# Down projection of a hybrid decoder layer: the low weight part from an accumulating GpSimd DMA in place of a VectorE subtraction

## Chip, cores and metric

One core of a Trainium2 chip runs the whole layer. The metric is the device time of one execution in microseconds (us); lower is better. "Before" is the kernel without the change.

## What is computed

The reference is one decoder layer over 512 tokens of width 1024 in float32: two attention branches with gates, an output projection, a gated MLP with a causal convolution, and per-layer embeddings. The change touches the MLP's last product, whose weight `w_down` is 2816 x 1024:

```
h = rmsnorm(x, mlp_pre_norm[i])
u = causal_dwconv(h @ w_up[i], conv_w[i], conv_b[i])
u_gate, u_val = jnp.split(u, 2, axis=-1)
ff = (jax.nn.gelu(u_gate, approximate=True) * u_val) @ w_down[i]
x = x + rmsnorm(ff, mlp_post_norm[i])
e = p[i] @ w_ple[i]
x = x + jax.nn.sigmoid(rmsnorm(x, ple_norm[i]) @ w_ple_gate[i]) * e
```

## The kernel before

Every large product is made in three passes of a reduced-precision type (fp32r): each operand is written as hi + lo, and `mm3` (line 75) issues hi*hi, hi*lo and lo*hi into the same bank of PSUM. An operand is split by `split` (line 71): ScalarE copies the float32 source into an fp32r tile (hi, line 72), and VectorE subtracts hi from the source into another fp32r tile (lo, line 73).

Weights come in chunks of 128 partitions x 1024 float32 (512 KB). `chunk` (line 133) takes a raw buffer, has SyncE (SP) issue the load (line 137), takes a hi and a lo buffer and calls `split`. The buffers stand in rings that are taken in turn (`wtile`, line 120): from line 672 on there are 3 raw, 4 hi and 4 lo buffers (lines 117 and 672 together). A raw buffer can be loaded again once its lo is made, since VectorE reads it; a hi or lo buffer can be written again once TensorE has made its last product with the chunk that was in it. Up projection, down projection and the gate of the embeddings all draw on these rings.

The down projection (`down_pass`, line 814) walks 11 chunks in each of three passes. Pass 0 makes the first 512 output columns for four blocks of 128 tokens: a chunk serves 2 x 4 x 3 = 24 products. Pass 1 makes the other 512 columns for blocks 0 and 1, pass 2 the same columns for blocks 2 and 3; each loads its 11 chunks anew, and there a chunk serves 12 products. So 33 chunks of `wd` are loaded. After pass 1 the norm of blocks 0 and 1 (`post_norm`, line 703) runs beside pass 2: ScalarE squares, VectorE scales and adds, and GpSimd makes the power of -1/2 (lines 710 and 102). `to_hT` (line 720) then transposes the blocks for the gate product, whose weights `wpg` come through `chunk` again (lines 837 and 840).

A scheduler orders each engine's instructions by priorities and its own estimate of time; on the chip each engine then works through its queue in that order, and an instruction that waits holds up all those behind it on its engine. GpSimd issues no DMA in this kernel.

Of the kernel before, what the change touches and what calls it, by code (L numbers as in the profile page):

```python
# [8 lines left out]
F32 = mybir.dt.float32  # L9
F32R = mybir.dt.float32r  # L10
I32 = mybir.dt.int32
AF = mybir.ActivationFunctionType
ALU = mybir.AluOpType
PSUM = bass.MemoryType.PSUM

P = 128
# [4 lines left out]
NPAIR = DFF // P  # L21
# [7 lines left out]

# columns of the per-partition parameter array  # L30
PP_QA, PP_KVA, PP_BG, PP_W0, PP_W1, PP_W2, PP_CB = 0, 2, 3, 19, 63, 107, 151
PP_N = 195
# columns of the constant array
CS_ID, CS_ONE, CS_SWA, CS_CAU, CS_INV = 0, 128, 256, 512, 1024
# [3 lines left out]
def hybrid_kernel(ctx, tc, T):  # L38
    nc = tc.nc
    act, dve, pool = nc.scalar, nc.vector, nc.gpsimd  # L40
    order = mybir.DependencyInfo(mybir.DependencyClass.NoSync, mybir.DependencyReason.DATA)

    class pe:
        """Products into one tile of PSUM keep their order."""
        last = {}
# [17 lines left out]
    def opened(**kw):  # L63
        cm = tc.tile_pool(reuse_waits="tile", **kw)
        p = cm.__enter__()
        return p, lambda: cm.__exit__(None, None, None)

    def f32(ap):
        return ap.bitcast(F32)

    def split(hi, lo, src):
        act.activation(hi, src, AF.Copy)  # L72
        dve.tensor_tensor(lo, src, f32(hi), ALU.subtract)  # L73
# [9 lines left out]

# [1 line left out]
    cpool, close_cpool = opened(name="cpool", bufs=1, side="left")  # L85
# [17 lines left out]

# [1 line left out]
    xp, close_xp = opened(name="xp", bufs=1, side="right")  # L105
# [9 lines left out]

    # rings of weights: pools with their buffers of each kind, taken in turn
    RA = (wa, {"raw": 2, "hi": 3, "lo": 2})
# [9 lines left out]

    # what is left of the first weights, then the outputs of the sliding window
    yt = yp.tile([P, 4, 1024], F32R, name="yt", tag="yt")
# [3 lines left out]
    def chunk(src, n=1024, parts=1, dst=None):  # L133
        raw = wtile("raw" if not W["slots"] or (W["raw"] + W["lo"]) & 2 == 0 else "lo", F32)
        w = n // parts
        for i in range(parts):
            nc.sync.dma_start(raw[:, i * w:(i + 1) * w], src[:, i * w:(i + 1) * w])
        hi = dst[0] if dst else wtile("hi", F32R)
        if dst:
            lo = dst[1]  # L140
        elif W["slots"]:
            lo = W["slots"].pop(0)
            W["slots"].append(lo)
        else:
            lo = wtile("lo", F32R)
        if parts == 1:
            split(hi[:, :n], lo[:, :n], raw[:, :n])
        else:
            for i in range(parts):
                u = slice(i * w, (i + 1) * w)  # L150
                dve.tensor_copy(hi[:, u], raw[:, u])
                dve.tensor_tensor(lo[:, u], raw[:, u], f32(hi[:, u]), ALU.subtract)
        return hi, lo

    def work(name="wkt"):
        return wk.tile([P, 1280], F32, name=name, tag="wkt", bufs=3)
# [13 lines left out]

# [1 line left out]
    psp, close_psp = opened(name="psp", bufs=1, space=PSUM)  # L172
# [11 lines left out]

    # the clock of the tensor engine rises while the first loads are on their way
    zeros = work("zeros")
    dve.memset(zeros[:, :P], 0.0)
    for _ in range(WARM):
        pe.matmul(psB[3][:, :P], zeros[:, :P], zeros[:, :P], start=True, stop=True)
    for k in range(8):  # L190
# [5 lines left out]
        if k % 2 == 0:  # L196
            hi, lo = chunk(T["wC"][k // 2], 768, 2 if k == 0 else 1)
        proj(psC, hi, lo, k, k % 2, 384)
    chB = [chunk(T["wB"][c], 576) for c in range(2)]
    nc.sync.dma_start(pp, T["pp"])  # L200
    # sigmoid(z) = (1 + tanh(z / 2)) / 2
    hb = cpool.tile([P, 16], F32, name="hb")
# [7 lines left out]

    # rstd of x, by token
    ssx = cpool.tile([P, NB], F32, name="ssx")
    rstd = cpool.tile([P, NB], F32, name="rstd")
# [3 lines left out]

# [1 line left out]
    posf = cpool.tile([P, NB], F32, name="posf")  # L219
# [25 lines left out]
    def rope(src, h, w, c, s2, a, b):  # L245
        """a + b is src (P, h, 2, w) rotated; c (P, w), s2 (P, 2, w)."""
        dve.tensor_tensor(a, src, c.unsqueeze(1).unsqueeze(1).to_broadcast([P, h, 2, w]), ALU.mult)
        for hf in range(2):
            dve.tensor_tensor(b[:, :, hf, :], src[:, :, 1 - hf, :],
                              s2[:, hf:hf + 1, :].to_broadcast([P, h, w]), ALU.mult)  # L250

    # rstd along the free axis, on every partition
    rbc = cpool.tile([P, S], F32, name="rbc")

    # q: rotate, transpose, split and stack
    St = sp.tile([P, 8, S], F32R, name="St", tag="sp")
# [18 lines left out]

    # k duplicated over the halves of the partitions
    khl = kvp.tile([P, 2, 2, S], F32R, name="khl", tag="kva")
# [32 lines left out]

# [1 line left out]
    def a_chunk(c):  # L312
# [3 lines left out]

    # norms of the latents
    ssc = cpool.tile([P, 2, NB], F32, name="ssc")
# [19 lines left out]

# [1 line left out]
    for c in range(4):  # L340
        hi, lo = chB[c] if c < 2 else chunk(T["wB"][c], 576)
# [8 lines left out]
    for t in range(3):  # L350
# [5 lines left out]
        dve.scalar_tensor_tensor(cqT[1][:, t, :], pt, g, f32(cqT[0][:, t, :]), ALU.mult, ALU.subtract)  # L356
    # rotary part of q, by token
    hi, lo = chunk(T["wuqp"], 512)
    qps = []
    for n in range(NB):  # L360
        ps = scT("psqp")
        b = slice(n * P, (n + 1) * P)
        for k in range(2):
            w = slice(k * 256, (k + 1) * 256)
# [6 lines left out]
    a_chunk(1)  # L371
    # rstd broadcast
    dg = work("dg")
# [23 lines left out]

# [1 line left out]
    ga = kvp.tile([P, 8, S], F32, name="ga", tag="ga")  # L399
# [33 lines left out]
    kT = qkp.tile([P, 8, S], F32, name="kT", tag="kT")[:96]  # L433
    # queries and keys of the latents: parts without rotation, transposed
    def latent_k(g):
# [21 lines left out]

    # shared rotary key: transpose, one copy for every head
    def latent_kr():
# [23 lines left out]

    # sliding window: a step is a block of queries and a kv head
    def swa_scores(n, g):
# [44 lines left out]

    # one pair of passes: the parts of v side by side, their outputs on the halves of the partitions
    def pv_mms(out, v, h, l, start, stop):
# [16 lines left out]

    # latent attention: a step is a head  # L550
    OFF = (0, 128, 384, 768)
# [58 lines left out]

    # values of the latent branch, by token
    vb = []
# [31 lines left out]

# [1 line left out]
    mxh = xp.tile([P, 8, S], F32R, name="mxh", tag="xh")  # L646
# [8 lines left out]
    for m in range(8):  # L655
# [3 lines left out]
        hi, lo = ch_b  # L659
        pb = p3[m]("pb")  # L660
        for k in range(4):
            w = slice((m % 2) * S + k * P, (m % 2) * S + (k + 1) * P)
# [14 lines left out]

# [1 line left out]

    pairs = [[accT, accT], [ptT, ptT], [scT, scT], [scT, pvT]]  # L680
# [59 lines left out]
    for blocks in ((0, 1), (2,), (3,)):  # L740
# [4 lines left out]
        if blocks == (2,):  # L745
            to_hT(0, ts[0])
            to_hT(1, ts[1])
# [1 line left out]
    ff = [xp.tile([P, 8, S], F32R, name="ff" + t, tag="x" + t) for t in "hl"]  # L749
# [23 lines left out]

    # the first two pairs by halves of the tokens
    chs = {j: [chunk(T["wup"][2 * j + gv]) for gv in range(2)] for j in range(2)}
# [22 lines left out]
    for j in range(2, NPAIR):  # L798
        if j in (8, 16):
            if j == 16:  # L800
                fp, close_fp = opened(name="fp", bufs=1, side="left")
            for l, t in ((ffh, "kT"), (ffl, "qT")):
                w = min(8, NPAIR - j)
# [10 lines left out]
    def down_pass(half, blocks):  # L814
        for c in range(NPAIR // 2):
            hi, lo = chunk(T["wd"][half * (NPAIR // 2) + c])
            for kk in range(2):
                k = 2 * c + kk
                w = slice(kk * S, (kk + 1) * S)
                for n in blocks:  # L820
                    b = slice(n * P, (n + 1) * P)
                    mm3(yd[n][half], ffh[k][:, b], ffl[k][:, b], hi[:, w], lo[:, w], k == 0, k == NPAIR - 1)
# [11 lines left out]

# [1 line left out]
    close_fp()  # L836
# [45 lines left out]
    raw = lp.tile([P, 1024], F32, name="wraw", tag="wraw", bufs=2)  # L882
    nc.sync.dma_start(raw, T["pT"].rearrange("p a b -> p (a b)"))
    split(ph.rearrange("p a b -> p (a b)"), pl.rearrange("p a b -> p (a b)"), raw)
    for k in range(2):
        raw = lp.tile([P, 1024], F32, name="wraw", tag="wraw", bufs=2)
        nc.sync.dma_start(raw, T["wp"][k])
        split(wph[:, k, :], wpl[:, k, :], raw)
    for n in range(NB):
        b = slice(n * P, (n + 1) * P)  # L890
        for half in range(2):
            ps = bank(2 + n % 2, "pe")
            w = slice(half * S, (half + 1) * S)
# [18 lines left out]
def layouts(i):  # L912
    """The inputs as the program takes them: slices, transposes and packing alone."""
    f = lambda a: np.ascontiguousarray(a)
    x = np.asarray(i["x"])[0]
# [5 lines left out]
    two = lambda w: w.reshape(4, 2, P, -1).transpose(0, 2, 1, 3).reshape(4, P, -1)  # L921
# [7 lines left out]
    wd = np.asarray(i["w_down"])[0].reshape(NPAIR // 2, 2, P, 2, 512).transpose(3, 0, 2, 1, 4)  # L929
# [5 lines left out]
    q, k = np.arange(P)[:, None], np.arange(P)[None, :]  # L935
# [64 lines left out]
```

## Time and profile before

| | us |
|---|---|
| median of 2 runs (760.22 to 761.43) | 760.83 |
| span of the profiled execution | 758.4 |
| TensorE busy | 748.5 (99%) |
| VectorE busy | 468.9 (62%) |
| ScalarE busy | 350.0 (46%) |
| GpSimd busy | 56.1 (7%) |

The span runs from the first to the last instruction of one profiled execution; the profiled execution has no time of its own besides it, so what lies around the span is taken as the difference to the median of the runs, 2.4 us. PE is TensorE, PEld its weight loads, DVE is VectorE, ACT ScalarE, POOL GpSimd, SP SyncE; L73 is line 73. The share of DMA is the mean busy share of 16 DMA engines.

### The profile page before, as it was taken

The page shows a single profiled execution, that of the slowest core. Times are in us where ns is not written, and L with a number is a line of the kernel's source. Part 1 is how long each engine was busy: PE and PEld are TensorE (multiplying, and loading weights), DVE is VectorE, ACT ScalarE, POOL GpSimd, SP SyncE. Part 2 cuts the span into 40 slices and gives each one's busy share as a digit, 9 for nine tenths or more (in the row PEclk, how much of TensorE's full clock was granted, in tenths as well). Part 3 has the DMA queues.
Part 4 walks back from the last instruction along what each step waited for, and adds up shares of the span by engine and source line. Part 5 has one row for each costly group of instructions (what it writes and reads, how often), then busy time and mean ns, then how long its engine had stood idle before and what let it go on. Part 6 is the DMA issues. An engine that isn't in the chain of part 4 may idle for free.

```text
span 758.4 us, 9410 instructions
## 1 busy us (share of the span) xinstructions
PE 748.5 (99%) x3562; PEld 615.6 (81%) x3562; DVE 468.9 (62%) x817; ACT 350.0 (46%) x610; POOL 56.1 (7%) x46
## 2 busy tenths in 40 slices
PE   9999999999999999999999999999999999999997
PEld 9988877778878778898888888888888888888886
DVE  6567788976785493848665655655654123486742
ACT  5833677755543243627434444344442123456531
POOL 0104023000000070110000000000000000011200
PEclk9999999999999999999999999999999999999999
DMA  8601221122122248224232232232322324556211
GB/s 308 245 30 63 60 84 42 62 79 58 54 84 63 76 132 312 74 95 139 84 100 95 84 111 84 92 103 84 111 84 86 110 83 140 194 180 212 81 55 56
DMA packets 25582, 81.28 MB, mean 107 GB/s; under 512 B 3297, under 2 KB 4577, under 8 KB 25537
## 3 DMA queue, kind: packets, MB, share of 16 engines
q1 hardware_dynamic: 25536, 80.68, 32.2%
q8 instruction: 28, 0.46, 0.3%
q14 instruction: 18, 0.14, 0.1%
HBM read 78.11 MB, written 2.10 MB: 106 GB/s over the span
## 4 chain that ended last, share of the span: by engine, by line
PE 92%; DVE 6%; issue 1%; ACT 0%; DVEq 0%
PE pu L56 30%; PE yd L56 16%; PE psg L56 11%; PE pg L56 6%; PE yo L56 5%; PE psba L56 3%; PE puh L56 3%; PE psA L56 3%; PE psC L56 2%; PE psB L56 2%; PE scm L56 2%; PE pe L56 1%; PE pb L56 1%; PE pvm L56 1%; PE ptm L60 1%
## 5 line engine op out<-in xcount | busy, mean ns | idle before, releaser
L73 DVE TENSOR_TENSOR wlo<-wraw,whi 128x1024 fp32r<-128x1024 f32 (+2 forms) x114 | 139.9, 1229 | 148.4 <-ACT whi L72 144.7
L56 PE MATMUL pu<-hT,whi 128*128 128x512 f32 x640 | 199.9, 393 | 0.0
L72 ACT ACTIVATE whi<-wraw 128x1024 fp32r<-128x1024 f32 (+4 forms) x120 | 123.1, 1026 | 164.5 <-PE yd L56 67.0
L56 PEld LDWEIGHTS pu<-hT,whi 128*128 128x128 f32 x640 | 120.1, 188 | 29.8
L56 PE MATMUL pu<-hT,wlo 128*128 128x512 f32 x320 | 127.7, 399 | 0.0
L56 PEld LDWEIGHTS pu<-hT,wlo 128*128 128x128 f32 x320 | 60.1, 188 | 13.9
L56 PE MATMUL psg<-xh,whi 128*128 128x512 f32 x128 | 51.7, 404 | 1.2 <-DVE ga L418 0.9
L56 PE MATMUL psg<-xl,whi 128*128 128x512 f32 x128 | 51.4, 402 | 0.0
L56 PE MATMUL psg<-xh,wlo 128*128 128x512 f32 x128 | 51.4, 402 | 0.0
L56 PE MATMUL yd<-whi,ffqT 128*128 128x512 f32 x112 | 43.7, 390 | 0.0
L56 PE MATMUL yd<-wlo,ffkT 128*128 128x512 f32 x112 | 43.6, 389 | 0.0
L56 PE MATMUL yd<-whi,ffkT 128*128 128x512 f32 x112 | 43.3, 389 | 0.0
L770 ACT ACTIVATE cv<-cv 128x512 f32<-128x512 f32 x22 | 13.9, 632 | 43.2 <-DVE cv L769 43.2
L710 POOL TENSOR_TENSOR q<-q,mhalf 128x1 f32<-128x1 f32 x8 | 5.3, 657 | 379.2 <-DVE q L709 378.9
L769 DVE SCALAR_TENSOR_TENSOR cv<-pu,pp,cv 128x510 f32<-128x510 f32 x40 | 30.0, 749 | 1.4
L767 ACT ACTIVATE cv<-pu,pp 128x512 f32<-128x512 f32 x40 | 30.5, 763 | 0.0
L56 PEld LDWEIGHTS psg<-xh,whi 128*128 128x128 f32 x128 | 24.1, 188 | 7.5 <-DVE ga L418 1.1
L768 DVE SCALAR_TENSOR_TENSOR cv<-pu,pp,cv 128x511 f32<-128x511 f32 x40 | 29.8, 745 | 0.0
L56 PEld LDWEIGHTS psg<-xl,whi 128*128 128x128 f32 x128 | 24.1, 188 | 5.4 <-issue 0.2
L56 PEld LDWEIGHTS psg<-xh,wlo 128*128 128x128 f32 x128 | 24.1, 188 | 5.4
L72 ACT ACTIVATE ffkT<-cv 128x512 fp32r<-128x512 f32 x14 | 8.8, 632 | 39.1 <-DVE cv L771 39.1
L56 PE MATMUL yd<-whi,ffl 128*128 128x512 f32 x64 | 25.4, 396 | 0.0
(264 smaller groups left out, 1484.1 us busy)
## 6 DMA issues: line engine op xcount, KB each, us to landing
wraw<-in_wup SPq DMA_DIRECT2D x44, 512.0 KB, 3.4
wraw<-in_wd SPq DMA_DIRECT2D x33, 512.0 KB, 3.4
wraw<-in_wg SPq DMA_DIRECT2D x16, 512.0 KB, 3.3
wraw<-in_wo SPq DMA_DIRECT2D x8, 512.0 KB, 4.6
wraw<-in_wpg SPq DMA_DIRECT2D x8, 512.0 KB, 3.9
xnat<-in_x SPq DMA_DIRECT2D x4, 512.0 KB, 7.0
wraw<-in_wba SPq DMA_DIRECT2D x4, 512.0 KB, 3.4
wraw<-in_wbb SPq DMA_DIRECT2D x4, 512.0 KB, 3.5
```

The costliest lines, as they stand in the source:

```text
L56: pe.chain(out, nc.tensor.matmul(out, *a, **k))
L60: pe.chain(out, nc.tensor.transpose(out, *a))
L72: act.activation(hi, src, AF.Copy)
L73: dve.tensor_tensor(lo, src, f32(hi), ALU.subtract)
L710: pool.tensor_tensor(r1, v, mhalf[:, :1], ALU.pow)
L767: act.activation(c, u, AF.Identity, scale=w2, bias=cb)
L768: dve.scalar_tensor_tensor(c[:, 1:], u[:, :S - 1], w1, c[:, 1:], ALU.mult, ALU.add)
L769: dve.scalar_tensor_tensor(c[:, 2:], u[:, :S - 2], w0, c[:, 2:], ALU.mult, ALU.add)
L770: act.activation(cs[0], cs[0], AF.Gelu_apprx_tanh)
```

## The change

In `down_pass` the call of `chunk` becomes a call of the new `chunk_acc`. The raw load and the making of hi are as before. For lo, ScalarE first writes -hi into the lo buffer, and then a DMA that GpSimd issues adds the chunk's source in HBM onto it. VectorE no longer takes part, and the raw buffer is read by ScalarE's copy alone. The 33 chunks of the three passes are made in this way; every other use of `chunk` is as it was. (The diff also takes out comments.)

```
+    def chunk_acc(src):
+        raw = wtile("raw", F32)
+        nc.sync.dma_start(raw, src)
+        hi, lo = wtile("hi", F32R), wtile("lo", F32R)
+        act.activation(hi, raw, AF.Copy)
+        act.activation(lo, f32(hi), AF.Copy, scale=-1.0)
+        pool.dma_start(lo, src, accum_op=ALU.add)
+        return hi, lo
...
     def down_pass(half, blocks):
         for c in range(NPAIR // 2):
-            hi, lo = chunk(T["wd"][half * (NPAIR // 2) + c])
+            hi, lo = chunk_acc(T["wd"][half * (NPAIR // 2) + c])
```

## Rows read from the trace of the kernel before

**Rows 1.** The page: busy time of each engine, and the chain that ended last.
```profile
PE 748.5 (99%) x3562; PEld 615.6 (81%) x3562; DVE 468.9 (62%) x817; ACT 350.0 (46%) x610; POOL 56.1 (7%) x46
...
PE 92%; DVE 6%; issue 1%; ACT 0%; DVEq 0%
```

**Rows 2.** Windows: passes 0, 1, 2 and the stretch behind them.
```profile
core 0: us, PE busy (x) PEld busy (x) DVE busy (x) ACT busy (x) POOL busy (x), PEclk, DMA share, GB/s
572.90:632.80 59.90, 59.90 (x262) 49.05 (x261) 16.43 (x16) 14.10 (x16) 0.00 (x0) 1.00 0.29 93
632.80:663.50 30.70, 30.70 (x135) 25.17 (x134) 13.71 (x13) 12.76 (x16) 0.00 (x0) 1.00 0.54 179
663.50:694.20 30.70, 30.70 (x143) 25.37 (x143) 22.25 (x28) 17.15 (x25) 2.94 (x4) 1.00 0.54 174
694.20:710.00 15.80, 15.80 (x69) 12.73 (x69) 14.41 (x17) 10.98 (x16) 6.36 (x3) 1.00 0.66 229
```

**Rows 3.** Groups of instructions in the three passes (572.9 to 694.2 us).
```profile
L73 DVE TENSOR_TENSOR wlo<-wraw,whi 128x1024 fp32r<-128x1024 f32 x32 | 39.1, 1225 | 64.8 <-ACT whi L72 64.8
L72 ACT ACTIVATE whi<-wraw 128x1024 fp32r<-128x1024 f32 x33 | 35.0, 1060 | 72.2 <-PE yd L56 67.0 <-DMA wraw<-in_wd 3.3 <-PE pu L56 1.1
```

**Rows 4.** Timeline of ScalarE in pass 0 and in pass 1.
```profile
606.49 1.06 ACT L72 ACTIVATE whi<-wraw 128x1024 fp32r<-128x1024 f32 x1 [4.38 <-PE yd L56]
611.93 1.06 ACT L72 ACTIVATE whi<-wraw 128x1024 fp32r<-128x1024 f32 x1 [4.38 <-PE yd L56]
...
647.66 1.06 ACT L72 ACTIVATE whi<-wraw 128x1024 fp32r<-128x1024 f32 x1 [1.66 <-PE yd L56]
650.38 1.06 ACT L72 ACTIVATE whi<-wraw 128x1024 fp32r<-128x1024 f32 x1 [1.66 <-PE yd L56]
```

**Rows 5.** Waits of the DMA queue (SP), 560 to 700 us.
```profile
SPq L137 <- DVE wlo L73: 121.9, 34, 5.4
```

**Rows 6.** The page: DMA issues, KB each and median us from issue to landing.
```profile
wraw<-in_wd SPq DMA_DIRECT2D x33, 512.0 KB, 3.4
...
xnat<-in_x SPq DMA_DIRECT2D x4, 512.0 KB, 7.0
```

**Rows 7.** DMA queues between 10 and 20 us, where many loads stand in the queue.
```profile
DMA packets 1882, 3.96 MB, mean 396 GB/s; under 512 B 336, under 2 KB 592, under 8 KB 1881
...
q1 hardware_dynamic: 1881, 3.95, 103.3%
```

**Rows 8.** Timeline of GpSimd, 660 to 700 us.
```profile
664.32 1.23 POOL L710 TENSOR_TENSOR q<-q,mhalf 128x1 f32<-128x1 f32 x2 [332.58 <-DVE q L709]
673.51 1.84 POOL L102 TENSOR_TENSOR q<-rs,mhalf 128x1 f32<-128x1 f32 x2 [7.96 <-DVE rs L101]
```

**Rows 9.** Windows: the norm of blocks 0 and 1 beside pass 2.
```profile
664.00:682.00 18.00, 18.00 (x84) 14.76 (x83) 15.07 (x19) 10.23 (x14) 2.94 (x4) 1.00 0.57 180
```

**Rows 10.** Timeline of the DMA queue: one issue on SP.
```profile
696.05 0.42 SPq L883 DMA_DIRECT2D wraw<-in_pT  x1
```

## The prediction

> **What bounds the kernel now.** I read the page's busy shares first, then the chain that ended last, then windows over the three passes, then who waits for whom there. TensorE is busy in 748.5 of 758.4 us and the chain is TensorE for 92% [rows 1]. In the windows, TensorE is busy without a gap in each pass, at a granted clock of 1.00, which is the 2.4 GHz level, while VectorE is busy for 16.4 of 59.9 us, 13.7 of 30.7 and 22.3 of 30.7 [rows 2]. So nothing that VectorE does here is waited for by TensorE. The groups agree: VectorE's subtraction for lo takes 1.225 us and sits idle before it until ScalarE's hi is there, and ScalarE's hi (1.06 us) sits idle for 67 us in all until TensorE has finished with a buffer [rows 3]. The weights are ahead, and the ring's buffers set the pace.
>
> The pace is read from ScalarE's timeline: a new hi is made every 611.93 - 606.49 = 5.44 us in pass 0 and every 650.38 - 647.66 = 2.72 us in passes 1 and 2 [rows 4]. That is what TensorE takes for the 24 and for the 12 products of a chunk. With four buffers, a chunk's hi and lo may be begun when the chunk four earlier is done, and TensorE comes to it three chunks later: it has 3 x 5.44 = 16.3 us in pass 0, but 3 x 2.72 = 8.2 us in passes 1 and 2.
>
> The resource that the change loads is the DMA. In passes 1 and 2 the 16 engines are already busy for 0.54 of the time and move 179 and 174 GB/s [rows 2].
>
> **What goes, and what it is worth.** 33 subtractions of 1.225 us leave VectorE, 40 us [rows 3]. TensorE waits for none of them, so I count zero. A gain is bounded at zero because TensorE has no gap in the passes, nor in the 15.8 us behind them [rows 2]. SP's wait for VectorE before it may load a raw buffer again, 121.9 us in sum [rows 5], ends earlier: the buffer comes free after ScalarE's copy. This too is worth nothing, since raw data hardly was what came last: 3.3 us of ScalarE's 72.2 us [rows 3].
>
> **What is added to ScalarE.** 33 writes of -hi, the same shape as hi, so 1.06 us each [rows 3], 35 us. Per chunk ScalarE then works 2.12 us. In pass 0 that lies in a gap of 4.38 us [rows 4]. In pass 1 it makes 12.76 + 11 x 1.06 = 24.4 of 30.7 us, in pass 2 17.15 + 11.7 = 28.8 of 30.7 [rows 2]. Beside the norm, where 18 us hold 10.23 us of ScalarE now [rows 9] and 6.6 chunks pass, it is 17.2 of 18. It fits at the old pace, barely; at a slower pace, which I expect, it is not the bound.
>
> **What is added to GpSimd.** 33 DMA issues. The trace has none, so I bound the issue by 0.42 us, one of SP's [rows 10], and by 2.72 us, beyond which it would itself set the pace of passes 1 and 2. I take GpSimd's mean instruction, 56.1 / 46 = 1.22 us [rows 1]. An issue waits for -hi, and behind it on GpSimd stand the powers of the norm [rows 8]; VectorE's norm of blocks 0 and 1 waits for these, but TensorE needs it only at the end of pass 2, so a few us late is free.
>
> **What is added to the DMA engines.** Per chunk 512 KB (0.524 MB) more are read from HBM, and since they are added onto what lies in SBUF, another 0.524 MB must be read there, with one write. An accumulating DMA does not occur in the trace. From below it costs like a plain load; from above I let one land before the next begins, at the slowest median landing of 512 KB, 7.0 us [rows 6]. Two rows give the rate of plain loads: 396 GB/s where many stand in the queue [rows 7], and 179 / 0.54 = 331 GB/s of busy engines where two do [rows 2]. I take the plain load at the full queue's rate, 0.524 / 0.396 = 1.32 us, and the accumulating one as two reads at the lower rate, 1.048 / 0.331 = 3.17 us, because its second read and its sum keep an engine from streaming at its best. Together 4.49 us of all engines per chunk. All three reads at 396 would be 3.97, all at 331 4.75.
>
> The Trainium skill says it differently: "DMA: Bandwidth & Descriptors", in "Anatomy of one DMA — SWDGE (gpsimd) path", fits a GpSimd DMA with 2.0 us plus its bytes over 436 GB/s. By that, an estimate from the page, ours would take 3.2 us, no more than the 3.4 us of the plain load of `wd` [rows 6], and two loads per chunk would keep the engines for 2.4 us, below 2.72: no change at all. The fit does not name the accumulation, and its rate is above the 396 GB/s that this trace reaches [rows 7]; the first rival below is this outcome, worked out from rows. The same page's "Rules for kernel authors" speaks against the change: an accumulating DMA reads its destination and writes it later. The trace before cannot show what this costs.
>
> **The sum.** In pass 0, 4.49 us of DMA per chunk stand below 5.44 of TensorE, and the way from a free buffer to a ready lo is 1.06 + 1.06 + 1.22 + landing. For the landing I take 5.2 us, between 3.4 and 7.0 [rows 6]: 8.5 us, below 16.3. Pass 0 stays as it is. In passes 1 and 2 the engines would need 4.49 us for what TensorE uses up in 2.72, so the DMA sets the pace. When pass 1 begins, its first three chunks are there or on the way, and the buffer for the fourth (chunk 14 of 33, counted from 0) comes free. Its lo is ready 8.5 us later; the 18 after it follow at 4.49 us, 80.8 us; the last needs 2.8 us of products: 92.1 us, in place of 61.4 (632.8 to 694.2 us) [rows 2]. The loss is 30.7 us, the span 789.1, and with the 2.4 us around it the time is 791 us.
>
> **The rivals.**
> First, no loss: an accumulating DMA keeps the engines as long as a plain load does. Then a chunk needs 1.048 / 0.396 = 2.65 us of DMA at the full queue's rate, less than 2.72, and the ring gives (8.5 + 2.72) / 4 = 2.8 us per chunk against 2.72. The time is 761, up to 769 with landings nearer 7 us: (10.3 + 2.72) / 4 = 3.26, half a us more on some of the 22 chunks, or ScalarE at 28.8 of 30.7 us slipping. This decides if the accumulating load takes under about 1.4 us of all engines. For it speaks that the 396 GB/s are shown [rows 7]; against it the second read.
>
> Second, the accumulating DMA is dearer still, for example because its parts don't overlap: with the 7.0 us of one landing per chunk, pass 0 is late as well, by 7.0 - 5.44 on some 8 chunks, 12 us, and passes 1 and 2 take 10.3 + 18 x 7 + 2.8 = 139 us, 78 more: 851 us. Nothing in the trace excludes it; a price between gives 800 to 850. TensorE's clock belongs here too: with 40% waiting in two passes it may be granted the 1.2 GHz level, of which these passes show nothing; a chunk's products would then take 5.44 us, which at the forecast pace costs up to 18 x 0.95 = 17 us more.
>
> Third, GpSimd's queue: if the powers of the norm are queued ahead of DMA issues, these stand still while the second power waits for VectorE. Now that is 7.96 us [rows 8], about the ring's whole slack of 8.2 us, of which the chain uses up 8.5. If the DMA engines are not the bound, this costs some 8 us once: 769. Against it: the two are independent, and the scheduler can place them either way.
>
> **How the numbers follow.** Forecast, the DMA engines set the pace of passes 1 and 2 at 4.0 to 4.8 us (782 to 797 by the same sum): 0.46. No loss or a few us: 0.17. Dearer than forecast: 0.31. GpSimd's order on top of cheap DMAs: 0.06. Two per cent, about what a measurement of this kernel can tell from no change, is 15 us, so slower begins at 776: 0.46 + 0.31 and a little of the third, 0.78. Same is 0.21. Faster over 2% would need 15 us from a TensorE that is idle for 10 us in the whole span [rows 1]: 0.01. The range reaches down into the cases without loss, 764, and up to the price of one landing per chunk, 855. The forecast's own range is 782 to 797.
>
> **What would show it.** In the windows of passes 1 and 2, TensorE has gaps, DMA share is near 1, and the passes last some 92 us together; pass 0 is unchanged at 60 us. TensorE waits for the accumulating DMA, not for ScalarE. If the share is far below 1 and TensorE still waits, it is the chain's length (landing, issue) and not the engines' time; if pass 0 is longer too, the second rival holds. If TensorE has no gaps, the DMA was as cheap as a plain load, and I was wrong in the second read.

## The result, and the profile after

The changed kernel takes 777.85 us against 760.83: the ratio is 1.0224, 95% interval 1.0205 to 1.0244, so 17 us slower. The profiled span grows from 758.4 to 776.0 us. The forecast was 791 us with a range of 764 to 855: the sign, the place and the mechanism came out, the size was 1.8 times too large. The time lies inside the range, but between two of its branches: "no loss" ends at 769 us and the forecast's own branch begins at 782. The time around the span is 1.8 us here (777.8 - 776.0), not the 2.4 that the forecast added.

The page of the kernel after: busy times, the two large DMA queues, the chain that ended last, and the new group and issue on GpSimd.

```profile
PE 753.2 (97%) x3562; PEld 613.8 (79%) x3562; DVE 430.0 (55%) x784; ACT 384.2 (50%) x643; POOL 80.2 (10%) x79
...
q1 hardware_dynamic: 25536, 80.68, 31.0%
q0 software_dynamic: 4752, 17.30, 12.4%
...
PE 83%; DMA 7%; DVE 6%; issue 2%; ACT 1%; SPq 0%; POOL 0%; DVEq 0%; POOLq 0%
...
L162 POOL DMA_DIRECT2D wlo<-in_wd x33 | 29.0, 878 | 336.6 <-ACT wlo L161 331.3
...
wlo<-in_wd POOLq DMA_DIRECT2D x33, 512.0 KB, 8.7
```

Against [rows 1], VectorE is 39 us less busy and ScalarE 34 us more, as the change has it, and a DMA has come into the chain with 7%. The queue q0 is new: 17.30 MB in 33 DMAs, 0.524 MB each, so the record counts an accumulating DMA's bytes once, whatever it reads at its destination. That matters for every GB/s below.

Where the time went is seen in windows over the passes, with the columns of [rows 2] (busy time and count of PE, PEld, DVE, ACT, POOL, then granted clock, DMA share, GB/s): pass 0, the beginning of pass 1, two stretches up to the end of the loads, and the last of the products.

```profile
572.90:632.80 59.90, 59.90 (x263) 49.05 (x262) 3.04 (x5) 25.65 (x28) 9.57 (x11) 1.00 0.90 192
632.80:646.00 13.20, 12.52 (x54) 9.77 (x52) 0.31 (x2) 10.41 (x14) 3.50 (x4) 1.00 0.91 209
646.00:672.50 26.50, 20.95 (x84) 15.22 (x84) 0.00 (x0) 14.17 (x14) 6.13 (x7) 1.00 1.06 275
672.50:703.60 31.10, 25.73 (x113) 19.30 (x112) 10.83 (x17) 22.07 (x31) 9.20 (x12) 1.00 1.06 278
703.60:717.80 14.20, 13.42 (x58) 10.63 (x57) 4.90 (x4) 4.91 (x6) 0.00 (x0) 1.00 0.80 231
```

Pass 0 is what it was, 59.9 us without a gap, though its DMA share rises to 0.90. From 646 us on TensorE is busy in 21 of 26.5 and in 26 of 31 us, where it had no gap, and the DMA share stands at 1.06. The clock stays at 1.00.

The waits behind the gaps, from the view of who waits for whom (engine, tile, line, waited for, us in total, times, longest), and the timeline of TensorE at two neighbouring chunks.

```profile
PEld yd L56 <- DMA wlo<-in_wd: 18.3, 14, 2.4
...
PE yd L56 <- DMA wlo<-in_wd: 12.4, 14, 2.0
```

```profile
654.94 0.50 PE L56 MATMUL yd<-wlo,ffkT 128*128 128x512 f32 x1 [0.81 <-DMA wlo<-in_wd]
...
658.70 0.50 PE L56 MATMUL yd<-wlo,ffkT 128*128 128x512 f32 x1 [0.75 <-DMA wlo<-in_wd]
```

TensorE's first product with lo waits for the accumulating DMA, chunk after chunk. A stall costs more than its 0.8 us of idle time: the waiting product itself takes 0.50 instead of 0.39 us, and each chunk loses about 1.1 us, as the pace shows. ScalarE's timeline gives it (compare the 2.72 us of [rows 4]); L160 is the write of hi.

```profile
649.93 1.06 ACT L160 ACTIVATE whi<-wraw 128x1024 fp32r<-128x1024 f32 x1 [2.88 <-PE yd L56]
...
653.71 1.06 ACT L160 ACTIVATE whi<-wraw 128x1024 fp32r<-128x1024 f32 x1 [1.63 <-PE yd L56]
...
657.53 1.06 ACT L160 ACTIVATE whi<-wraw 128x1024 fp32r<-128x1024 f32 x1 [1.68 <-PE yd L56]
...
661.32 1.06 ACT L160 ACTIVATE whi<-wraw 128x1024 fp32r<-128x1024 f32 x1 [1.64 <-PE yd L56]
...
668.94 1.06 ACT L160 ACTIVATE whi<-wraw 128x1024 fp32r<-128x1024 f32 x1 [1.64 <-PE yd L56]
```

From 649.93 to 668.94 us five chunks pass, 3.80 us each. Counted as three streams of 0.524 MB (raw load, the accumulating DMA's source, its destination), that is 414 GB/s. The DMA queues between 650 and 690 us, first, and between 585 and 632 us in pass 0, second (queue: packets, MB, share of 16 engines; then KB each and us from issue to landing):

```profile
q0 software_dynamic: 1507, 5.49, 68.7%
q1 hardware_dynamic: 1520, 5.54, 36.9%
...
wlo<-in_wd POOLq DMA_DIRECT2D x10, 512.0 KB, 10.1
```

```profile
q0 software_dynamic: 1215, 4.39, 58.3%
...
wlo<-in_wd POOLq DMA_DIRECT2D x9, 512.0 KB, 5.9
```

Per chunk the accumulating DMA keeps all engines for 0.687 x 3.80 = 2.6 us, the raw load for 1.4; the two shares sum to more than 1, so these times overlap a little. In pass 0 a DMA lands 5.9 us after its issue, in passes 1 and 2 after 10.1. A share is not a need: in pass 0 the engines count as busy for 0.90 x 5.44 = 4.9 us per chunk, though 3.80 us are enough for a chunk where they are full.

### The profile page after: what moved, and what is told of

Same layout as the page of the kernel before. It is cut to its first block, busy times and chain, and to the rows that moved or that the text cites. A ratio compares the mean times of both kernels' runs of the same rounds, so it can differ in the third digit from the quotient of the medians.

```text
span 776.0 us, 9487 instructions
## 1 busy us (share of the span) xinstructions
PE 753.2 (97%) x3562; PEld 613.8 (79%) x3562; DVE 430.0 (55%) x784; ACT 384.2 (50%) x643; POOL 80.2 (10%) x79
## 3 DMA queue, kind: packets, MB, share of 16 engines
q0 software_dynamic: 4752, 17.30, 12.4%
## 4 chain that ended last, share of the span: by engine, by line
PE 83%; DMA 7%; DVE 6%; issue 2%; ACT 1%; SPq 0%; POOL 0%; DVEq 0%; POOLq 0%
PE pu L56 29%; PE yd L56 11%; PE psg L56 11%; DMA wlo<-in_wd 6%; PE pg L56 5%; PE yo L56 5%; PE psba L56 3%; PE puh L56 3%; PE psA L56 3%; PE psC L56 2%; PE psB L56 2%; PE scm L56 2%; PE pe L56 1%; PE pb L56 1%; PE pvm L56 1%
## 5 line engine op out<-in xcount | busy, mean ns | idle before, releaser
L73 DVE TENSOR_TENSOR wlo<-wraw,whi 128x1024 fp32r<-128x1024 f32 (+2 forms) x81 | 99.5, 1231 | 97.8 <-ACT whi L72 94.1
L72 ACT ACTIVATE whi<-wraw 128x1024 fp32r<-128x1024 f32 (+4 forms) x87 | 88.2, 1014 | 99.4 <-PE pu L56 27.8
L56 PE MATMUL pu<-hT,wlo 128*128 128x512 f32 x320 | 125.4, 392 | 0.0
L162 POOL DMA_DIRECT2D wlo<-in_wd x33 | 29.0, 878 | 336.6 <-ACT wlo L161 331.3
L160 ACT ACTIVATE whi<-wraw 128x1024 fp32r<-128x1024 f32 x33 | 35.0, 1059 | 56.8 <-PE yd L56 51.1
L56 PE MATMUL yd<-whi,ffkT 128*128 128x512 f32 x112 | 41.4, 390 | 0.0
L56 PEld LDWEIGHTS yd<-wlo,ffkT 128*128 128x128 f32 x112 | 21.0, 188 | 18.2 <-DMA wlo<-in_wd 14.0
L161 ACT ACTIVATE wlo<-whi 128x1024 fp32r<-128x1024 f32 x33 | 34.9, 1059 | 0.8
```

Source lines behind the costliest of these rows:

```text
L56: pe.chain(out, nc.tensor.matmul(out, *a, **k))
L160: act.activation(hi, raw, AF.Copy)
L161: act.activation(lo, f32(hi), AF.Copy, scale=-1.0)
L162: pool.dma_start(lo, src, accum_op=ALU.add)
```

## The experiments

Theory E, the forecast's: the 16 DMA engines are full with three streams per chunk and set the pace. Its rivals: ScalarE's added writes (S), HBM (H), and the way of a single buffer from free to ready, divided by four buffers (C). C deserves respect: 2.5 us from the beginning of hi to the DMA's issue, 10.1 to land and 2.7 of products, (2.5 + 10.1 + 2.7) / 4, is 3.8 as well. The question is whether 10.1 us is what such a DMA takes, or the time that it stands in line. All edits are against the changed kernel but for the last control.

**VectorE adds, no DMA.**

```
-        pool.dma_start(lo, src, accum_op=ALU.add)
+        dve.tensor_tensor(lo, raw, f32(lo), ALU.add)
```

> Keeps ScalarE's write of -hi, but VectorE adds the raw buffer onto it in place of the accumulating DMA. Theory E (the 16 DMA engines, with three streams per chunk, set the pace): the loss is gone, 761 us (760 to 763). Rival S (ScalarE's 33 added writes, 35 us, are what costs): the loss stays in part, 766 us or more.

760.82 us, ratio 1.0002 (0.9992 to 1.0011). ScalarE's 35 us cost nothing; S falls, and the whole loss comes with the DMA.

**The accumulating DMA in pass 0 alone.**

```
-            hi, lo = chunk_acc(T["wd"][half * (NPAIR // 2) + c])
+            hi, lo = (chunk if half else chunk_acc)(T["wd"][half * (NPAIR // 2) + c])
```

> The accumulating DMA in pass 0 alone (11 chunks of 33); passes 1 and 2 as before. Theory E: a chunk of pass 0 has 5.44 us and the DMA needs 3.8, so no loss, 761 us (760 to 762.5). Rival (a cost per accumulating DMA wherever it stands): a third of the 17 us, 766 to 767 us.

760.69 us, ratio 0.9998 (0.9989 to 1.0008). Eleven of the 33 DMAs are free where a chunk has 5.44 us. The loss is made in passes 1 and 2.

**A plain GpSimd DMA of the same bytes.**

```
-        pool.dma_start(lo, src, accum_op=ALU.add)
+        pool.dma_start(lo, src)
```

> GpSimd's DMA writes the source into lo instead of adding it (lo is then the weight itself, not its low part): same issue, same queue, same waits, one read per element less. Theory E: two streams per chunk, 1.049 MB at some 400 GB/s = 2.6 us against 2.72, no loss beyond a us or two, 761 to 764 us. Rival C (the chain of one buffer, with a landing of 10 us that a GpSimd DMA takes by itself, divided by four buffers): 3.8 us per chunk as it is, 777 us.

763.69 us, ratio 1.0041 (1.0028 to 1.0054). Its DMA between 650 and 690 us:

```profile
DMA packets 3838, 13.99 MB, mean 350 GB/s; under 512 B 427, under 2 KB 427, under 8 KB 3837
...
wlo<-in_wd POOLq DMA_DIRECT2D x13, 512.0 KB, 5.2
```

Same queue, same waits, same write, no accumulation: 14 of the 17 us are gone. So the accumulation makes the loss. What it adds is a read of the destination and the addition itself, and no run separates these two. The issue takes 0.55 us here where it took 0.88; GpSimd has room for either. What is left, 3 us, was not traced to one wait. Two streams at 350 GB/s are 3.0 us per chunk, not the 2.6 that was expected, against TensorE's 2.72, and in passes 1 and 2 TensorE waits for this DMA once, 1.1 us.

**No raw loads.** The raw load is made once per pass, and its buffer serves all 11 chunks.

```
+    kept = []
...
+    def chunk_acc(src, first):
+        if first:
+            kept[:] = [wtile("raw", F32)]
+            nc.sync.dma_start(kept[0], src)
+        raw = kept[0]
...
+            hi, lo = chunk_acc(T["wd"][half * (NPAIR // 2) + c], c == 0)
```

> The raw load is made once per pass and its buffer used for all 11 chunks (30 of 33 raw loads are left out, hi is that of the first chunk); the accumulating DMAs stay. Theory E: only the accumulating DMA's share is left, about 2.6 us of all engines per chunk, below 2.72: 761 to 764 us, and landings near the 5.9 us of pass 0. Rival C (landing of 10 us by itself): 3.8 us per chunk, 777 us.

762.62 us (one run). Between 650 and 690 us:

```profile
q0 software_dynamic: 1897, 6.90, 93.6%
...
wlo<-in_wd POOLq DMA_DIRECT2D x14, 512.0 KB, 5.6
```

The accumulating DMA alone lands in 5.6 us while TensorE goes at nearly its full pace, and it keeps the engines for 0.936 x 40 / 13.2 = 2.8 us per chunk (6.90 MB are 13.2 of them), a little above the 2.6 expected and about TensorE's 2.72. So 10.1 us is not what such a DMA takes by itself: in the changed kernel nearly half of it is time in line with the raw loads.

**The source in SBUF.** The accumulating DMA takes the norm's gain as its source.

```
-    def chunk_acc(src):
+    def chunk_acc(src, g_post):
...
-        pool.dma_start(lo, src, accum_op=ALU.add)
+        pool.dma_start(lo, g_post, accum_op=ALU.add)
```

> The accumulating DMA takes its source from a tile in SBUF (the gain of the norm, 512 KB) instead of the weight in HBM; lo is then not the low part. Same bytes through the engines, half the bytes from HBM. Theory E (the engines set the pace): unchanged, 776 to 779 us, 3.8 us per chunk. Rival H (HBM sets it, with 1.049 MB per 3.8 us): one stream from HBM is left, 761 to 765 us.

779.23 us (one run). Between 650 and 690 us:

```profile
q0 software_dynamic: 1522, 5.52, 69.4%
...
wlo<-gain POOLq DMA_DIRECT2D x10, 512.0 KB, 10.1
```

Half the bytes from HBM, and share, landing and time are close to those of the changed kernel. H falls; the engines are what is full. Whether the limit lies in the engines themselves or on the SBUF side that all streams share was not separated.

**Three hi buffers instead of four.**

```
-        hi, lo = wtile("hi", F32R), wtile("lo", F32R)
+        hi, lo = wa.tile([P, 1024], F32R, name="whi", tag="whi", bufs=3), wtile("lo", F32R)
```

> The hi buffers of the down projection taken from three instead of four, so at most three chunks are under way. Theory E: the engines still set the pace, about 3.8 us per chunk, the landing falls to some 6 us, 777 to 782 us. Rival C (landing of 10 us by itself): (2.5 + 10 + 2.7) / 3 = 5.1 us per chunk, some 19 us more, 795 us or above.

802.93 us (one run): theory E missed here, and C's number came, though C's landing of 10 us did not. The page's busy times, windows over three stretches of passes 1 and 2, and ScalarE's timeline:

```profile
PE 765.2 (96%) x3562; PEld 625.5 (78%) x3562; DVE 428.5 (53%) x784; ACT 385.1 (48%) x643; POOL 80.4 (10%) x79
...
646.00:672.00 26.00, 19.64 (x70) 15.28 (x71) 0.00 (x0) 11.55 (x11) 4.36 (x5) 0.87 0.97 239
672.00:700.00 28.00, 21.69 (x86) 16.80 (x85) 9.62 (x15) 17.71 (x25) 8.34 (x11) 0.88 0.90 217
700.00:730.00 30.00, 20.54 (x70) 15.76 (x69) 1.39 (x3) 12.03 (x13) 4.32 (x5) 0.78 0.89 215
```

```profile
651.97 1.06 ACT L160 ACTIVATE whi<-wraw 128x1024 fp32r<-128x1024 f32 x1 [5.01 <-PE yd L56]
...
654.75 1.06 ACT L160 ACTIVATE whi<-wraw 128x1024 fp32r<-128x1024 f32 x1 [0.63 <-PE yd L56]
...
657.47 1.06 ACT L160 ACTIVATE whi<-wraw 128x1024 fp32r<-128x1024 f32 x1 [0.57 <-PE yd L56]
...
662.44 1.06 ACT L160 ACTIVATE whi<-wraw 128x1024 fp32r<-128x1024 f32 x1 [2.83 <-PE yd L56]
...
669.62 1.06 ACT L160 ACTIVATE whi<-wraw 128x1024 fp32r<-128x1024 f32 x1 [5.04 <-PE yd L56]
```

The DMA is no longer full: it moves 215 to 239 GB/s as counted, where the changed kernel has 275 (the share alone, 0.89 to 0.97, would not say so). The chunks come in bunches, four in 669.62 - 651.97 = 17.65 us, 4.4 us each, and between the bunches the engines run dry. The median landing between 650 and 690 us is 7.8 us, and (2.5 + 7.8 + 2.7) / 3 = 4.3: with three buffers the ring is too short to keep the engines full, and C's formula describes the pace with this landing. On top, the granted clock falls to 0.78 to 0.88. The 25 us divide by the busy times: TensorE is busy 765.2 - 753.2 = 12 us longer with the same 3562 products, and idle for the other 13; 4.4 - 3.8 us on 22 chunks is 13 as well. Without the 12 us the time would be some 791 us, an estimate from these rows, between E's 782 and C's 795: C's number came in part by the clock, which neither had in its sum.

**The control: three hi buffers in the kernel before.**

```
-        hi = dst[0] if dst else wtile("hi", F32R)
+        hi = dst[0] if dst else wa.tile([P, 1024], F32R, name="whi", tag="whi", bufs=3) if hi3 else wtile("hi", F32R)
...
-            hi, lo = chunk(T["wd"][half * (NPAIR // 2) + c])
+            hi, lo = chunk(T["wd"][half * (NPAIR // 2) + c], hi3=True)
```

> The kernel before (VectorE subtracts) with three hi buffers in the down projection, the control for the three-buffer run. If three buffers cost nothing while a lo is ready 2.3 us after its buffer comes free (2 x 2.72 = 5.4 us of slack), 761 us, and the 25 us that three buffers added to the changed kernel come from the accumulating DMA's longer way; if three buffers are short by themselves, 765 us or more.

760.89 us (one run). Where lo is ready some 2.3 us after its buffer comes free, three buffers cost nothing.

**More buffers in passes 0 and 1.** Eight hi and lo buffers instead of four; pass 2 has the four.

```
+    ex = [hp.tile([P, 4, 1024], F32R, name=f"ex{i}", tag=f"hT{i}") for i in range(2)]
...
+            dst = [t[:, i % 4, :] for t in ex] if i < 22 and i % 8 >= 4 else None
+            hi, lo = chunk_acc(T["wd"][half * (NPAIR // 2) + c], dst)
```

> Four more hi and lo buffers in passes 0 and 1 (in the tiles that hold the transposed activations before and after), so that pass 0's spare DMA time (5.44 - 3.8 us per chunk, 11 chunks) can make chunks ahead. Theory E: DMA work is unchanged but some 4 chunks of it move into pass 0, worth 3.8 us each: 761 to 767 us. Rival C (the chain of a buffer, four deep): pass 1 free of loss, pass 2 as it is, about 769 us.

767.29 us, ratio 1.009 (1.0073 to 1.0107), 0.3 us over E's range. The DMA in pass 0 (585 to 632 us), and two windows: the later part of pass 1 with the beginning of pass 2, then the rest of pass 2:

```profile
q0 software_dynamic: 1821, 6.61, 71.5%
...
ex<-in_wd POOLq DMA_DIRECT2D x6, 512.0 KB, 13.2
wlo<-in_wd POOLq DMA_DIRECT2D x5, 512.0 KB, 16.4
```

```profile
646.00:672.50 26.50, 26.50 (x116) 21.55 (x115) 5.72 (x10) 14.21 (x18) 6.63 (x9) 1.00 1.05 265
672.50:703.60 31.10, 26.81 (x121) 20.67 (x120) 8.70 (x11) 17.81 (x22) 5.76 (x7) 1.00 0.97 252
```

The time alone does not tell E from C, since 767 and 769 were expected; the landings do. With twice the buffers the DMAs land after 13 to 16 us, and still 6.61 MB pass in 47 us, one per 3.73 us. More under way, same pace: the engines are full, and time in line grows. The spare DMA time of pass 0 does buy chunks ahead: pass 1 has no gap, and what is left of the loss stands in pass 2.

**Part of the columns.** The accumulating DMA makes the first 768 (or 512) of 1024 columns of lo, VectorE subtracts the rest.

```
-        act.activation(lo, f32(hi), AF.Copy, scale=-1.0)
-        pool.dma_start(lo, src, accum_op=ALU.add)
+        act.activation(lo[:, :768], f32(hi[:, :768]), AF.Copy, scale=-1.0)
+        pool.dma_start(lo[:, :768], src[:, :768], accum_op=ALU.add)
+        dve.tensor_tensor(lo[:, 768:], raw[:, 768:], f32(hi[:, 768:]), ALU.subtract)
```

> The accumulating DMA makes three quarters of lo's columns, VectorE's subtraction the fourth quarter. Theory E: 0.524 + 0.75 x 1.049 = 1.311 MB per chunk through the engines at 414 GB/s, 3.17 us, so 0.45 us of loss per chunk in place of 1.08: 767 to 770 us. A loss that hangs on the number of DMAs and not on their bytes would stay at 777 us.

> The accumulating DMA makes half of lo's columns, VectorE's subtraction the other half. Theory E: 0.524 + 0.5 x 1.049 = 1.049 MB per chunk at 414 GB/s is 2.53 us, below 2.72: 761 to 764 us, as with the plain GpSimd DMA of the same bytes. If the loss went with the number of accumulated bytes (17 us for all, 9 us for three quarters), it would be some 4 us or more: 765 us.

Three quarters: 769.61 us (one run), with a hi every (665.85 - 649.80) / 5 = 3.21 us in ScalarE's timeline, where 3.17 was expected.

```profile
649.80 1.06 ACT L160 ACTIVATE whi<-wraw 128x1024 fp32r<-128x1024 f32 x1 [2.31 <-PE yd L56]
...
665.85 1.06 ACT L160 ACTIVATE whi<-wraw 128x1024 fp32r<-128x1024 f32 x1 [1.27 <-PE yd L56]
```

Half: 762.44 us, ratio 1.0028 (1.0016 to 1.0041). The loss is not proportional to the accumulated bytes, 17 us, 9 and then 1.6. It nearly vanishes where the DMA time of a chunk, 2.53 us as expected here, comes below TensorE's 2.72. A quarter of the accumulated bytes is worth 3.80 - 3.21 = 0.59 us, so all of them 2.4.

No version beats the kernel before: TensorE has no gap there for any of them to close.

## Why the prediction was right, and where its size was off

Right, by the steps of the forecast:

- VectorE's 40 us were worth nothing, and the earlier release of the raw buffers too: TensorE waited for neither, and the loss came with both gone.
- ScalarE's writes are free (VectorE adds: 1.0002), and GpSimd's issue is: it takes 0.878 us, where 1.22 was taken between bounds of 0.42 and 2.72. The third rival, the norm's powers in GpSimd's queue, did not occur: TensorE's longest wait for the DMA, 2.0 us, stands at 647.32 us, 26 us before the first of these powers (673.12).
- Pass 0 has the slack that the ring gives it: 59.9 us as before, and no loss from the DMA in pass 0 alone.
- The DMA engines set the pace of passes 1 and 2, from chunk 15 on. The landing taken, 5.2 us, is near the 5.9 of pass 0, but where the engines are full it is 10.1.

The term that was mis-sized is the price of the accumulating DMA, "two reads at the lower rate, 1.048 / 0.331 = 3.17 us". It measured 2.4 us (3.80 less the raw load's 1.4), and by the shares 2.6. The reason given, that a second read keeps an engine from streaming, does not hold: with the accumulation counted as two reads, it and the raw load together run at 414 GB/s, a little above the 396 of a full queue of plain loads [rows 7]. All three streams at that rate was worked out as the lower bound, 3.97 us, and set aside; 3.80 was measured. So the pace lies just below the forecast's own band of 4.0 to 4.8 us, and it is the wide range that holds the time. The lower rate of [rows 2], 331 GB/s, is no limit, since more loads at once reach more; it came from dividing by a share below 1, which overstates the need, as pass 0 above shows. With 3.80 the forecast's own formula gives 8.5 + 18 x 3.80 + 2.8 = 79.7 us for the stretch.

Measured, from the beginning of pass 1 to the last product of the down projection, the stretch is 717.8 - 632.8 = 85.0 us. In it lie 21 products of the gate, 4.9 us (707.66 to 710.47 and 713.20 to 715.30 us in TensorE's timeline), which the scheduler set between the last chunks; before, they stand behind the stretch. Less them it is 80.1. That this is so near to 79.7 is in part luck. The first lo that comes late, chunk 15's, is used 14.5 us after pass 1 begins (647.32 us), where the formula has 8.5 + 3.80 = 12.3; and the gate's products lie in part in time that would have been waited through, so taking off all of their 4.9 us makes the rest look shorter. A second, small slip: before, the last product of the down projection ends at 696.0 and not at 694.2 us, since the transposes of blocks 0 and 1 lie within pass 2; the stretch to compare with is 63.2 and not 61.4 us. 80.1 - 63.2 = 16.9, and the span grew by 17.6.

The first rival, no loss, is what a plain GpSimd DMA nearly does (1.0041). The Trainium skill's fit for a GpSimd DMA ("DMA: Bandwidth & Descriptors", "Anatomy of one DMA — SWDGE (gpsimd) path") gave 3.2 us for 512 KB, an estimate: the accumulating one lands in 5.9 us in pass 0 and in 5.2 there with no raw load beside it, so the fit does not hold for it. The plain one takes 4.6 us in pass 0, more than the estimate as well. The same page says that an accumulating DMA reads its destination ("Rules for kernel authors"). The runs agree in the size, with 2.4 to 2.8 us of engine time against 1.4 for a plain load, from HBM or from SBUF, but they do not show the read by itself.

## What to carry to other kernels

Count an accumulating DMA as about two plain loads of its bytes (1.7 to 2 here), and set the sum of all streams, at the rate of a full queue, against what the consumer takes per tile. Well below that the DMA is free (pass 0), close below it costs a little (1.6 us with half of the columns), above it every tile pays the difference. Landing times in a loop say little: with full engines they grow with the buffers under way, and only a rate that stays when buffers are added shows what is full. Work taken off an engine that nobody waits for is worth nothing, and here it was paid for with DMA time, of which passes 1 and 2 had too little to spare.

## What was not expected of the hardware

The accumulating DMA costs the engines no more than two reads would: 2.4 us of all 16 per 512 KB by the pace, 2.6 to 2.8 by the shares, against 1.4 for a plain load beside it, and reading the source from SBUF instead of HBM changes nothing at this load. And the granted clock held at 1.00, the 2.4 GHz level, while TensorE idled for about a fifth of the time from 646 to 703.6 us in waits of at most 2.0 us. It fell to a mean of 0.78 to 0.88 in the run with three buffers, where the longest wait is 3.8 us and TensorE is idle for 23 to 32% of the windows shown; products take up to 793 ns there, against a median of 389. What draws the line between these two cases is not shown. The forecast had allowed up to 17 us for the clock; in the changed kernel it cost nothing.
